# TensorE's instructions pinned to the order of the source in a three-block transformer kernel

## The chip, the cores and the metric

The program runs on one core of one Trainium2 chip. The metric is the device time of one execution in microseconds (us). It is launched once, takes its inputs from HBM and leaves one output of 256 x 1024 fp32 there. The engines are called by the profile's names: PE is TensorE's matmul, PEld its weight loads, DVE VectorE, ACT ScalarE, POOL GpSimd, and SP the queue that issues nearly all loads. "LIN" is used below for the matmuls of lines 217 to 219.

## The reference, cut to what matters

All of it is fp32, batch 1, 256 tokens, model width 1024. A first block takes `x` and a modulation vector:

```python
hn = _rmsnorm(h, norm1_g) * (1.0 + scale1) + shift1
y_ssm = _mamba2_mixer(hn @ w_z, hn @ w_xbc, hn @ w_dt, ...) @ w_ssm_out      # chunked scan, 32 heads
y_nsa = _nsa_mixer(hn @ w_q, hn @ w_kc, ..., hn @ w_gn, ...) @ w_nsa_out     # compressed, selected, window branch
merged = jax.nn.sigmoid(hn @ w_gs) * y_ssm + jax.nn.sigmoid(hn @ w_ga) * y_nsa
h = h + gate1 * (merged @ w_o)
hn2 = _rmsnorm(h, norm2_g) * (1.0 + scale2) + shift2
h = h + gate2 * _hier_moe(hn2, ...)                                          # 32 experts, 2 for each token
```

Two more layers follow on that result. Layer 0 is grouped-query attention with a context stream of 256 tokens of its own and a gated feed-forward part (2816 wide, with a convolution of three taps). Layer 1 is latent attention with a second feed-forward part. A last norm gives the output. The modulation vectors of all layers are products of a silu-ed vector with wide matrices (`w_ada`, `ada_w`).

## The kernel before, in words

**Products.** Weights are fp32 in HBM. `split_weight` (L188) loads 256 KB pieces into the ring `raw` (14 buffers), ACT rounds a piece to `whi` (L198), DVE takes the rest `wlo` (L199), four buffers each. `mm3` (L214) then makes three matmuls for each product: `whi` by hi (L217), `wlo` by hi (L218), `whi` by lo (L219). `lin_fm` (L221) yields after each 24 of these, `lin_tm` (L247) after 12 wider ones or so. Products with the modulation weights (`ada_quad`, L385) go straight from `raw` in fp32: one unit is eight matmul records of L391, in four column tiles.

**How the stages are written.** Each stage is a Python generator that yields the cost of a unit. `weave` (L137) traces units of side chains among the units of a main one, by shares: beside `tanh_gates` (L1012) go the scan `ssd` (share 0.7, then 0.6), the sparse attention `nsa` (0.35) and the modulation (0.3); beside `ssd_gate` the sparse attention (0.55). `drain` traces what is left of a chain with nothing beside it. So the source has an order: the order in which instructions are traced. Between two yields a generator's instructions stand together, with nothing of another chain among them.

**What orders the instructions.** Tile's scheduler takes the traced program, keeps the data dependencies, and gives each engine an order of its own by a model of the times: where the next instruction in the source's order is not ready by that model, a later one goes first. PE's sequence in the profile is thus not the source's. PSUM is cut into rings by `banks` (L122): in the first block `aux` has two banks.

**Places that the prediction speaks of**, in the order of the program:

- `first_block` (L1021): `project_tm` (L581) is the second projection; then `project_xbc` with `nsa_prepare`.
- `ssd` (L654): for each of four groups and two chunks, transposes (L685), two pairs of matmuls (L704, L705), L713 or L722 and L728, and L735. L704 and L705 are followed by an exponential (L707, ACT) and a product (L708, DVE) that L735 reads. The last one and a half of its eight rounds are drained before the z projection.
- `nsa_compress` (L830) ends in one unit with L855, L864, L873, L880, each reading what DVE made of the one before. `nsa_cmp_probs` (L887) is one unit: L894, a copy, transposes L900, a softmax on DVE and ACT (L901 to L917), transposes L921.
- `nsa_attend` (L925): scores L941, transposes L973, products L980 and L986. Its last 15 units are drained after the z projection (L1053), then comes the product with `w_nsa_out` beside `ssd_norm` (L764; L769, a chain on DVE and POOL, L519).
- `layer0_ctx_in` (L1651): `load_fm` loads 1 MB of the context into the buffer that the last `y_lo` leaves, and transposes it (L362). This is traced after the last product with `w_ssm_out` and before the first with `w_o` (L1079 to L1083).
- `square_sums`, `rstd_bcast`, `spread` (L477 to L521): a norm, as L489 (sums of squares), a copy (L492), L494, DVE, POOL (L507), DVE (L516), L519, all in one unit.
- `router`, `experts` (L1093, L1381), beside them the context's attention; `experts_rest` (L1396) is a conditional block.
- `layer0_x_attend` (L1690): `final_norm`, projections, heads (L1571), attention (L1710, L1490, L1498).
- `layer1_x` (L1828): `mla_in`, twice two `mla_norm` (L1738: ACT, DVE, POOL, DVE, then transposes L1751), `mla_kv_heads` (L1794) and `mla_q_heads` (L1812), beside them the attention (L1848).
- The feed-forward parts are plain runs of `lin_fm`; `finish` (L1869) is the last norm.

Of the kernel before, what the change touches and what calls it, by code (L numbers as in the profile page):

```python
# [79 lines left out]
# The quads of ada columns that are made beside the router and beside layer 0's attention.  # L80
Q2, Q3 = (0,), (1, 2)
# The rings that hold weights loaded ahead for the experts, before and after the phase's buffers are free.
ROOM = ("raw", "k4"), ("raw", "k4", "Q", "raw", "k4")
# How much of a side chain goes beside each step of the main one.
# [4 lines left out]
# The experts by their rank in number of tokens: the order of the units (rank of group, half) and their blocks.  # L89
# [3 lines left out]
# The 8 KB buffers: those of the second part lie where what the first part keeps there is done early.  # L93
# [5 lines left out]
class Kernel:  # L99
# [21 lines left out]
    @contextmanager  # L121
    def banks(self, **bufs):  # L122
        """The eight PSUM banks, cut into rings for one part of the program."""
        with self.tc.tile_pool(name="psum", bufs=1, space=bass.MemoryType.PSUM, reuse_waits="tile") as self.psum:
            self.psum_bufs = bufs
            yield

    @contextmanager
    def phase(self, **bufs):
        """Buffers that live for one part of the program."""  # L130
        with self.tc.tile_pool(name="phase", bufs=1, reuse_waits="tile") as p:
            self.phase_pool, self.phase_bufs = p, bufs
            yield
        self.phase_pool, self.phase_bufs = None, {}

    @staticmethod
    def weave(main, *fills):  # L137
        """main with units of each (generator, share) among its own, by their TensorE time. A fill that yields None
        waits for main."""
        done, spent = 0.0, [0.0] * len(fills)  # L140
        for cost in main:
            yield cost
            done += cost
            for i, (g, share) in enumerate(fills):
                while spent[i] < share * done:
                    try:
                        c = next(g)
                    except StopIteration:
                        spent[i] = float("inf")
                        break  # L150
                    if c is None:
                        spent[i] = share * done
                        break
                    spent[i] += c
                    yield c
# [14 lines left out]
    def passing(self, name, tag):  # L170
        """A constant that is needed only once."""
        which, a, n = self.cst_at[name]
        t = self.sb(tag, [P, n], name=name)
# [8 lines left out]
    # ---------------------------------------------------------------- weights  # L182
# [5 lines left out]
    def split_weight(self, view):  # L188
        """(hi, lo) of each block of 128 rows of a view [128, n, cols]."""
# [14 lines left out]
    def flush(self):  # L204
        """Evictions are traced after the next weights' split, which TensorE waits for."""
# [15 lines left out]
    def lin_fm(self, W, c0, ncols, act, evict, k0=0, nk=None, more=False):  # L221
        """out^T: features on partitions. W [K, N] in DRAM; act (hi, lo) [128, nk, 256]."""
# [24 lines left out]
    def lin_tm(self, W, c0, ncols, act, evict, chunk=512):  # L247
        """out: tokens on partitions."""
# [25 lines left out]
    # ---------------------------------------------------------------- set-up  # L274
# [73 lines left out]
    def load_fm(self, src, h, tag, eng):  # L348
        """[256, 1024] rows of DRAM -> feature-major h [128, 8, 256]."""
# [16 lines left out]
    # ---------------------------------------------------------------- adaLN  # L366
# [11 lines left out]
    def take_bias(self, stg, dst):  # L378
        """The bias into dst [128, slots, 48], to which the products are added."""
# [5 lines left out]
    def ada_quad(self, W, q, dst, rsel):  # L385
        """Columns 2048q..2048q+2047 of silu(c) @ W onto dst [128, slots, 48]."""
# [17 lines left out]
    def ada_start(self, p):  # L404
        """Shift and scale of the first norm for half of the features, in the order of ada1."""
# [20 lines left out]
    def first_act(self, rb):  # L426
        """The first norm and the first two chunks of the token-major projection, by halves of the features as the
        modulation comes in."""
# [47 lines left out]
    # ---------------------------------------------------------------- norms  # L476
    def square_sums(self, h, nt, st, gain=None):  # L477
        """Sums of squares over features (32 times them) into the two columns of st: the column tiles of TensorE add up
        a quarter each."""
# [17 lines left out]
    def rms_bcast(self, h, nt, dim):  # L497
        """1/rms over features, one column per token, on all partitions (PSUM [128, 256])."""
# [11 lines left out]
    def spread(self, r, n):  # L510
        """Columns of r, one value per token, along the free dimension of all partitions."""
# [11 lines left out]
    def modulation(self, gain, ada, slot, vs, vsc):  # L523
        """gain * (1 + scale) and shift, [128, 8] each."""
# [15 lines left out]
    # ---------------------------------------------------------------- first block: projections  # L540
# [26 lines left out]
    def rope(self, x, nh, t, outs):  # L567
        """x [128, nh, 64] token-major, half-split rotation; written to each of outs."""
# [12 lines left out]
    def project_tm(self, act, pss):  # L581
        """dt, q, k/v, gates of the first block, tokens on partitions; the first two chunks are in pss."""
# [8 lines left out]
    def conv_silu(self, dst, ps, wname, bname, m, nm, taps):  # L591
        """Causal depthwise convolution over tokens, then silu."""
# [20 lines left out]
    # ---------------------------------------------------------------- SSD  # L613
# [40 lines left out]
    def ssd(self):  # L654
        """The chunked scan; y (with the skip) replaces the x channels. Yields where TensorE would wait."""
# [90 lines left out]
    def ssd_gate(self, act, sums):  # L746
        """y * silu(z), and its squares summed by group into sums [2][128, 2, 256]."""
# [35 lines left out]
    # ---------------------------------------------------------------- NSA  # L783
# [141 lines left out]
    def nsa_attend(self):  # L925
        """Selected and window branches (causal both: every block is chosen and the window spans the sequence)."""
# [79 lines left out]
    # ---------------------------------------------------------------- first block  # L1006
    def sigmoid(self, out, x):
        """By tanh, whose table is the exponential's too."""
# [3 lines left out]
    def tanh_gates(self, act, c0, sg):  # L1012
        """tanh(x / 2): the sigmoid is half of one more."""
        def ev(m, ps):
            self.A.activation(sg[:, m, :], ps, AF.Tanh, scale=0.5)
        yield from self.lin_fm(self.I["w_in"][0], c0, D, act, ev)

# [3 lines left out]
    def first_block(self, rb):  # L1021
        V, A, T, I = self.V, self.A, self.T, self.I
        h = self.h
        act, pss = self.first_act(rb)
        self.mark("tm")
# [66 lines left out]
    # ---------------------------------------------------------------- mixture of experts  # L1092
    def router(self, h):  # L1093
# [35 lines left out]
        def top(x):  # L1129
            """softmax over the 8 columns; its sorted values and their places."""  # L1130
# [55 lines left out]
        # experts by their number of tokens: place of each expert and expert of each place  # L1186
# [67 lines left out]
    def one_hots(self, d, cols):  # L1254
        """For positions 256 d + cols: token x position, by first and second choice, [128, 2, n] per half of tokens."""
# [10 lines left out]
    def expert_gather(self, d, tag, n=256):  # L1266
        """The normalised tokens at positions 256 d.., features on partitions."""
# [15 lines left out]
    def expert_weights(self, part, experts):  # L1283
        """One part of the experts' weights, 256 rows of gate or up or 256 columns of down each."""
# [21 lines left out]
    def expert_block(self, xg, d, q, experts, sizes):  # L1306
        """The 128 positions 256 d + 128 q..: one expert's, or several experts' in the column tiles of TensorE."""
# [42 lines left out]
    def expert_spread(self, d, q):  # L1350
        """What takes the block's rows back to the tokens, position x token, and the rows' weights."""
# [29 lines left out]
    def experts(self):  # L1381
        """The two experts with the most tokens have 128 positions each, the next two 64, the others 32."""
# [13 lines left out]
    def experts_rest(self):  # L1396
        """Tokens beyond those positions: blocks of 32 from position 1536."""
# [8 lines left out]
    def final_norm(self, h, gain, mod, tag):  # L1406
        """The next norm (hi, lo) of h normalised with its gain, and what brings h itself there."""
# [8 lines left out]
        # with m the mean square of h, the mean square s / m of the normalised h, plus eps, times m: both norms at once  # L1416
# [17 lines left out]
    # ---------------------------------------------------------------- second block  # L1434
    def axial(self, x, nh, cos, sin, out):
        """x [128, nh, dim] token-major -> out; cos, sin [128, dim] (signs and gains inside)."""
# [13 lines left out]
    def attend(self, S_fn, V_fn, nkt, scale, hi, lo, s_tag, o_tag, ready=None, room=None):  # L1450
        """Softmax attention of 16 heads in pairs, 256 queries; out^T into (hi, lo). Scores run two steps ahead."""
# [87 lines left out]
    def gqa_heads(self, pr, is_x, c0, nh, t_done):  # L1539
        """Norm and rotation of the heads in columns c0.. of pr, by halves of the tokens; t_done(t, c0) takes them."""  # L1540
# [34 lines left out]
    def gqa_project(self, act, is_x, qT, kT, tags):  # L1575
        """Keys and values first; each piece's heads are finished under the next piece's products."""
# [161 lines left out]
    def mla_norm(self, src, col, n, gain, dst, t0):  # L1738
        """rms-normalised columns, transposed to features on partitions with the gain; dst (hi, lo)."""
# [17 lines left out]
    def mla_in(self, act, col0, n):  # L1757
        """Columns col0.. of the products into latents, by halves of the tokens."""
# [7 lines left out]
    def mla_latent(self, pin, is_x):  # L1766
        """Normed latent (transposed) and shared keys from the 288 columns of keys and values."""
# [13 lines left out]
    def mla_kv_heads(self, ck, kr, c, is_x, vm, kc):  # L1781
        """Keys and values of heads 4c.. into kTm, vm; kc [128, 2, 4, 96] is room for the keys."""
# [86 lines left out]
    def finish(self):  # L1869
        """The last norm, tokens on partitions."""  # L1870
# [22 lines left out]
    def run(self):  # L1893
        with self.tc.tile_pool(name="sb", bufs=1) as self.pool:
# [26 lines left out]
            with self.phase(k4=4, m=3, fg=2, hT=2):  # L1921
                with self.banks(lin=2, S=2, aux=2, acc=2):
# [10 lines left out]
                    self.mark("experts rest")  # L1933
                    self.experts_rest()
                with self.banks(lin=4, fl=1, aux=2, acc=1):
# [9 lines left out]
                    self.drain(self.layer1_x())  # L1945
                    self.finish()
# [31 lines left out]
```

## Time and profile before

| | before |
|---|---|
| times of three runs | 1762.91, 1765.79, 1771.38 us; median 1765.79 |
| span of the profiled execution | 1765.9 us |
| PE busy, share of the span | 1690.6 us, 96% |
| PEld busy | 1379.4 us, 78% |
| DVE busy | 1272.3 us, 72% |
| ACT busy | 917.8 us, 52% |
| HBM read | 378.00 MB, 215 GB/s over the span |
| mean granted TensorE clock | 0.981 |

The page gives no time of the profiled execution beside its span; the span is 0.1 us above the median of the runs. PE counts as busy while any matmul record is open, and the records overlap: a LIN matmul of 256 columns has a record of 0.28 us and the next one starts 0.12 us after it, so a short wait between two matmuls can lie inside a busy stretch. [...]

### The profile page before, as it was taken

The page shows a single profiled execution, that of the slowest core. Times are in us where ns is not written, and L with a number is a line of the kernel's source. Part 1 is how long each engine was busy: PE and PEld are TensorE (multiplying, and loading weights), DVE is VectorE, ACT ScalarE, POOL GpSimd, SP SyncE. Part 2 cuts the span into 40 slices and gives each one's busy share as a digit, 9 for nine tenths or more (in the row PEclk, how much of TensorE's full clock was granted, in tenths as well). Part 3 has the DMA queues.
Part 4 walks back from the last instruction along what each step waited for, and adds up shares of the span by engine and source line. Part 5 has one row for each costly group of instructions (what it writes and reads, how often), then busy time and mean ns, then how long its engine had stood idle before and what let it go on. Part 6 is the DMA issues. An engine that isn't in the chain of part 4 may idle for free. (4 is left out here: it accounts for less than half of the span.)

```text
span 1765.9 us, 36466 instructions
## 1 busy us (share of the span) xinstructions
PE 1690.6 (96%) x12980; PEld 1379.4 (78%) x12980; DVE 1272.3 (72%) x3070; ACT 917.8 (52%) x1901; POOL 42.4 (2%) x48
## 2 busy tenths in 40 slices
PE   7999999999999999999999898999999989999998
PEld 3898777767876578888887554688999866789997
DVE  3997687675667768757756466968777788777876
ACT  2666446863443544534434252656665566556654
POOL 0000000100001000000000001000000000000000
PEclk8999999999999999999999988999999999999999
DMA  9756956849966997998999886234566432246662
GB/s 321 212 150 195 322 175 191 253 133 306 317 201 207 323 318 240 329 328 268 325 347 346 258 299 229 90 122 138 178 183 183 141 120 72 59 141 183 180 186 72
DMA packets 344962, 381.54 MB, mean 216 GB/s; under 512 B 27353, under 2 KB 298454, under 8 KB 344774
## 3 DMA queue, kind: packets, MB, share of 16 engines
q1 hardware_dynamic: 339456, 376.47, 67.2%
q10 hardware_dynamic: 5174, 1.97, 0.4%
q8 instruction: 104, 1.70, 0.4%
q0 software_dynamic: 144, 0.71, 0.1%
q14 instruction: 84, 0.69, 0.1%
HBM read 378.00 MB, written 1.05 MB: 215 GB/s over the span
## 5 line engine op out<-in xcount | busy, mean ns | idle before, releaser
L198 ACT CAST whi<-raw 128x512 fp32r<-128x512 f32 (+2 forms) x752 | 453.9, 610 | 383.9 <-PE lin L219 219.5
L199 DVE TENSOR_TENSOR wlo<-raw,whi 128x512 fp32r<-128x512 f32 (+2 forms) x752 | 502.4, 678 | 161.5 <-ACT whi L198 148.6
L217 PE MATMUL lin<-XA,whi 128*128 128x256 f32 x768 | 220.1, 287 | 1.7 <-ACT XA L465 1.7
L219 PE MATMUL lin<-XA,whi 128*128 128x256 f32 x768 | 219.0, 286 | 0.0
L218 PE MATMUL lin<-XA,wlo 128*128 128x256 f32 x768 | 218.9, 285 | 0.0
L217 PE MATMUL lin<-A,whi 128*128 128x256 f32 x576 | 168.4, 292 | 2.7 <-DVE k L598 1.9
L218 PE MATMUL lin<-A,wlo 128*128 128x256 f32 x576 | 163.5, 284 | 0.0
L217 PEld LDWEIGHTS lin<-XA,whi 128*128 128x128 f32 x768 | 149.3, 194 | 2.6 <-ACT XA L465 2.5
L218 PEld LDWEIGHTS lin<-XA,wlo 128*128 128x128 f32 x768 | 149.2, 194 | 0.7 <-issue 0.4
L219 PEld LDWEIGHTS lin<-XA,whi 128*128 128x128 f32 x768 | 148.9, 194 | 0.3
L217 PEld LDWEIGHTS lin<-A,whi 128*128 128x128 f32 x576 | 109.9, 191 | 33.8 <-issue 14.1
L219 PE MATMUL lin<-A,whi 128*128 128x256 f32 x448 | 127.7, 285 | 0.0
L217 PE MATMUL lin<-CA,whi 128*128 128x256 f32 x416 | 122.0, 293 | 0.3 <-ACT whi L198 0.2
L218 PE MATMUL lin<-CA,wlo 128*128 128x256 f32 x416 | 118.2, 284 | 1.1 <-DVE wlo L199 1.1
L219 PE MATMUL lin<-CA,whi 128*128 128x256 f32 x416 | 117.9, 283 | 0.0
L218 PEld LDWEIGHTS lin<-A,wlo 128*128 128x128 f32 x576 | 110.1, 191 | 0.9 <-issue 0.7
L1621 ACT ACTIVATE cv<-lin,vecs 128x256 f32<-128x256 f32 x132 | 73.9, 560 | 63.0 <-PE lin L219 52.7
L219 PE MATMUL lin<-XB,whi 128*128 128x256 f32 x352 | 99.4, 286 | 0.1
L1622 DVE SCALAR_TENSOR_TENSOR cv<-lin,vecs,cv 128x255 f32<-128x255 f32 x132 | 63.3, 480 | 49.4 <-ACT cv L1621 49.1
L217 PE MATMUL lin<-XB,whi 128*128 128x256 f32 x352 | 98.7, 283 | 0.0
L218 PE MATMUL lin<-XB,wlo 128*128 128x256 f32 x352 | 98.4, 283 | 0.0
L217 PEld LDWEIGHTS lin<-CA,whi 128*128 128x128 f32 x416 | 79.2, 190 | 15.5 <-issue 6.5
(534 smaller groups left out, 3835.0 us busy)
## 6 DMA issues: line engine op xcount, KB each, us to landing
raw<-in_ffn_w_up_dram SPq DMA_DIRECT2D x264, 256.0 KB
raw<-in_ada_w_dram SPq DMA_DIRECT2D x192, 256.0 KB
raw<-in_ffn_w_down_dram SPq DMA_DIRECT2D x132, 256.0 KB
raw<-in_w_in_dram SPq DMA_DIRECT2D x112, 256.0 KB
wx<-in_w_exp_gate_dram SPq DMA_DIRECT2D x112, 256.0 KB
wx<-in_w_exp_up_dram SPq DMA_DIRECT2D x112, 256.0 KB
wx<-in_w_exp_down_dram SPq DMA_DIRECT2D x112, 256.0 KB
raw<-in_w_ada_dram SPq DMA_DIRECT2D x96, 256.0 KB
```

The costliest lines, as they stand in the source:

```text
L198: self.A.copy(hi, raw)
L199: self.V.tensor_tensor(lo, raw, hi.bitcast(F32), OP.subtract)
L217: mm(out, whi, ahi, start=first, stop=False, skip_group_check=True)
L218: mm(out, wlo, ahi, start=False, stop=False, skip_group_check=True)
L219: mm(out, whi, alo, start=False, stop=last, skip_group_check=True)
L1621: A.activation(acc, ps, AF.Identity, bias=self.v(f"fb{i}", m), scale=self.v(f"fw{i}1", m))
L1622: V.scalar_tensor_tensor(acc[:, 1:], ps[:, 0:TOK - 1], self.v(f"fw{i}0", m), acc[:, 1:], OP.mult, OP.add)
```

## The change

A method `pin` opens and closes a region in which the scheduler has to issue PE's instructions in the order in which they were traced. The other engines' orders, and the DMA queues', stay the scheduler's. The region opens after `first_act`, ahead of the second projection, is closed around the conditional block `experts_rest`, and ends ahead of `finish`. No unit, share, buffer or operation differs. The diff takes out the comments and docstrings too; these lines are left out here.

```diff
+    def pin(self, on=True):
+
+        if on:
+            self.pinned = self.tc.manual_schedule(engines={mybir.EngineType.PE})
+            self.pinned.__enter__()
+        else:
+            self.pinned.__exit__(None, None, None)
...
         act, pss = self.first_act(rb)
+        self.pin()
         self.mark("tm")
...
                     self.mark("experts rest")
+                    self.pin(False)
                     self.experts_rest()
+                    self.pin()
...
                     self.mark("L1")
                     self.drain(self.layer1_x())
+                    self.pin(False)
                     self.finish()
```

## Rows read from the trace of the kernel before

**Rows 1.** The page, by engine: busy us, share of the span, instructions.
```profile
PE 1690.6 (96%) x12980; PEld 1379.4 (78%) x12980; DVE 1272.3 (72%) x3070; ACT 917.8 (52%) x1901; POOL 42.4 (2%) x48
```
**Rows 2.** Windows: stretch, length, PE, PEld, DVE, ACT, POOL busy us (count), clock, DMA share, GB/s.
```profile
44.10:1721.80 1677.70, 1622.51 (x12482) 1327.93 (x12481) 1228.32 (x2970) 884.82 (x1838) 40.05 (x41) 0.98 0.69 217
1280.30:1324.40 44.10, 44.10 (x370) 44.10 (x369) 34.48 (x68) 28.03 (x54) 0.00 (x0) 1.00 0.61 183
```
**Rows 3.** Timeline of PE, first block: start, us, line, out<-in, tile shape, form, count.
```profile
187.45 0.64 PE L848 MATMUL acc<-raw,blk 128*32 128x128 f32 x16
187.91 1.02 PE L391 MATMUL fl<-raw,stat 128*32 128x512 f32 x2
188.86 0.50 PE L704 MATMUL aux<-k,tri_r 128*128 128x512 f32 x1
189.29 1.06 PE L391 MATMUL fl<-raw,stat 128*32 128x512 f32 x6
190.28 0.39 PE L217 MATMUL lin<-A,whi 128*128 128x256 f32 x1
...
212.90 1.06 PE L391 MATMUL fl<-raw,stat 128*32 128x512 f32 x8
213.90 0.38 PE L217 MATMUL lin<-A,whi 128*128 128x256 f32 x1
```
**Rows 4.** Timelines of SP and PE, the context's load.
```profile
474.58 0.37 SPq L354 DMA_DIRECT2D x_tm<-in_ctx_dram  x1
...
479.79 0.71 PE L362 MATMUL aux<-ident,x_tm 128*128 128x128 f32 x5
```
**Rows 5.** Timeline of PE, two norms; in brackets the idle time before, and its releaser.
```profile
488.79 0.67 PE L519 MATMUL aux<-k,ones 128*128 128x256 f32 x2 [0.34 <-DVE k L516]
...
1409.71 0.61 PE L494 MATMUL aux<-ones,sqsum 128*128 128x1 f32 x4 [0.53 <-DVE sqsum L492]
1411.96 1.19 PE L519 MATMUL aux<-k,ones 128*128 128x256 f32 x2 [1.65 <-DVE k L516]
```
**Rows 6.** Timeline of PE, the compressed branch's softmax; window of the tile scmp: DVE, ACT busy.
```profile
230.60 0.38 PE L900 MATMUL aux<-ident,scmpT 128*128 128x128 f32 x2
...
238.10 0.44 PE L921 MATMUL aux<-ident,scmp 128*128 128x128 f32 x2
...
231.00:238.10 7.10, 0.00 (x1) 0.01 (x1) 3.93 (x7) 0.63 (x1) 1.00 0.80 256
```
**Rows 7.** Windows of line L217 alone: stretch, length, PE busy (count), PEld busy.
```profile
271.10:285.80 14.70, 3.98 (x13) 2.45 (x13) 1.00 0.65 196
359.00:388.00 29.00, 2.71 (x9) 1.70 (x9) 1.00 0.36 112
```
**Rows 8.** Windows of line L391 alone.
```profile
271.10:285.80 14.70, 3.17 (x16) 0.45 (x16) 1.00 0.65 196
359.00:388.00 29.00, 2.10 (x8) 0.29 (x8) 1.00 0.36 112
```
**Rows 9.** Timelines of ACT and PE, layer 1's latents.
```profile
1423.38 0.40 ACT L1762 COPY pin<-lin 128x288 f32<-128x288 f32 x1
1426.31 0.30 PE L1751 MATMUL aux<-ident,junk 128*128 128x128 f32 x1 [0.66 <-DVE junk L1747]
...
1433.55 0.48 ACT L1762 COPY pin<-lin 128x384 f32<-128x384 f32 x1
1436.73 0.33 PE L1751 MATMUL aux<-ident,junk 128*128 128x128 f32 x1 [0.38 <-DVE junk L1747]
```
**Rows 10.** Waits of PE: who for whom, us in total, times, longest.
```profile
PE acc L1339 <- DVE hT L1328: 2.9, 4, 1.8
```
**Rows 11.** Windows, as in Rows 2, around falls of the granted clock.
```profile
1005.00:1011.16 6.16, 4.57 (x38) 2.12 (x36) 3.04 (x8) 0.69 (x1) 0.00 (x0) 1.00 0.03 9
1011.16:1028.23 17.07, 12.69 (x52) 4.56 (x54) 5.10 (x15) 8.67 (x19) 1.66 (x2) 0.50 0.70 237
1410.52:1417.35 6.83, 4.27 (x14) 3.44 (x15) 4.45 (x11) 2.15 (x5) 0.70 (x1) 0.50 0.02 6
```

## The prediction

> **What bounds the kernel now.** I read the page's busy times first, then the windows, then the waits and timelines. PE is busy for 1690.6 of 1765.9 us, the next engine, DVE, for 72% [rows 1]. From the second projection's stretch to the last slice it is busy for 1622.5 of 1677.7 us [rows 2]: the sum of all its visible waits there is 55.2 us. Removing every wait could not win more than that, while added ones have no such end. The feed-forward parts show what a stretch without waits looks like: busy for 44.1 of 44.1 us [rows 2]. They are plain runs of one generator with nothing beside it, so their order is the source's already; those 380 us or so neither win nor lose.
>
> Three things in the rows show that PE's order is not the source's. L391's unit of eight is cut in 2 and 6 with L704 between [rows 3]. LIN of the z projection and L391, 3 x 13 matmuls and 16 records, run inside the last rounds of the scan, which the source drains with nothing beside them [rows 7, 8]. LIN of the next product fill the time until the context has landed, which the source puts behind it [rows 4]. The amount of PE's work stays; what the change alters is how much of it lies under other engines' chains. PE waits at the first instruction in the source's order that isn't ready, and all behind it wait too. So I go through the places where the source has a chain with no other PE work between its links and the trace has some.
>
> **The change part by part.** The sum is against the profiled execution, 1765.9 us, which is the median of the runs within 0.1 us.
>
> *Context load.* The DMA goes out at 474.58, when the last product that reads its buffer's old content is through, and L362 starts at 479.79 [rows 4]: 5.2 us, filled with LIN of `w_o`. In the source L362 stands ahead of those. PE stands for the whole latency: **+5.2**. [...]
>
> *Norms.* Without cover L494 waits 0.53 and L519 1.65 us [rows 5]: 2.2 us that the source has in every norm, for a norm is one unit. With the cover that the scheduler found, L519 waits 0.34 [rows 5]. There are six covered places: the context's first norm, the router's, the scan's, the context's in its feed-forward part, the final norm and the context's in layer 1, 1.6 to 1.9 us each: **+10** (5 to 13).
>
> *Compressed branch.* L900 ends at about 231.0, L921 starts at 238.1 [rows 6]. In these 7.1 us PE had LIN, L391 and scores to do. The chain's own work on that tile is 3.93 us of DVE and 0.63 of ACT [rows 6], 4.6; with three small operations on its sums and the passages between engines, which the rows of the norm show to add a few tenths each, I take 5.5. L855 to L880 and the two L894-to-L900 passages before it are four more round trips of 0.5 to 0.7 (the 0.53 of [rows 5] is one). Together **+8** (5 to 10).
>
> *Scan.* In the last rounds, 14.7 us long, 39 LIN at 0.12 (4.7) and 16 L391 (3.2) lie between the links [rows 7, 8]; 7.9 us of later work, which the source has behind them. The chains (exponential, product, the two banks of `aux`) need part of it: I take 4. Six rounds woven into the gate projections have two or three of the scan's units in a row; half to one us each for the bank to come free, 4 in all. **+8** (0 to 15).
>
> *Sparse attention's drain.* Between 359 and 388, 27 LIN (3.2) and 8 L391 (2.1) are pulled ahead [rows 7, 8]. The last 15 units follow each other in the source: **+5** (0 to 6).
>
> *Latents of layer 1.* From the eviction's start to the first transposes are 2.9 us (1423.38 to 1426.31) and 3.2 us (1433.55 to 1436.73), of which 0.66 and 0.38 show as waits, the rest is LIN of the next products [rows 9]. In the source nothing stands there, so +2.3 and +2.8; the second halves of the tokens and the transposes of the first heads, with the same kind of chain, I put at 4 more, the three further rounds of heads at 1 each: **+12** (6 to 18).
>
> *Router, experts, grouped-query heads.* L1339 waits 2.9 us in four of its ten blocks [rows 10]; a few LIN after L1357 hide it in the others. 0.5 us each there, 3 for the heads' chain ahead of L1571. The experts' weights come at full DMA load, so part may cost nothing: **+6** (0 to 15).
>
> *What goes.* A run of two L391 takes 0.95 us (187.91 to 188.86) and the other six 0.99, an undivided unit of eight 1.00 [rows 3]. A cut costs 0.94 us. Counted along PE's timeline there are some 85 runs for 64 units ([rows 3] shows one cut); 12 of the cuts lie where PE was not waiting anyway: −11 (0 to −20). Waits that the scheduler's order itself made: −3. **−14**.
>
> *Clock.* After the stretch in which PE was busy for 4.57 of 6.16 us the granted clock fell to 0.50 for 17.1 us; inside the norm of [rows 5], after PE had stood twice, for 6.8 us [rows 11]. These are two of seven such stretches between 1000 and 1570. Five of the new waits are of that size (context load, softmax, the two latents, one drain). A stretch of 6.8 us at half the clock costs at most 3.4 if PE works all through; in this one it was busy for 4.27 of 6.83. I take 2 each: **+10** (0 to 25).
>
> Sum: 5.2 + 10 + 8 + 8 + 5 + 12 + 6 = 54.2; less 14, plus 10: **+50**, 1816 us. No DMA is issued by PE, SP's order stays, and `raw` runs up to 14 pieces ahead; loads are late only where PE frees buffers late. While PE stands, ACT and DVE can round at most two units of weights ahead (four buffers of `whi`), and where PE is the bound that gives nothing back. Around the norms DVE is what is late next.
>
> [...] The rows give 0.94 us for a cut of L391, and L848's 16 records, in column tiles too, take 0.46 (187.45 to 187.91) in front of L391 [rows 3]. [...]
>
> **The rivals.**
>
> *Whole units win* (faster). All 20 cuts join (−19), the source's LIN units of 24 (2.9 us) cover most chains, and of the waits only the context load and the softmax stay (+11); with −10 of the scheduler's own misplaced waits out of the 55.2: about −18, 1748 us. For it: the source does put a LIN unit between most links. Against it: the places above have none. It decides from the point where the added waits are under 25 us.
>
> *Nothing to measure* (flat). The scheduler takes the source's order where it can, so the orders are close; added 25, saved 20: 1770. For it: most LIN groups stand whole in the timeline. Against: the 39 LIN and 16 L391 in the scan's end.
>
> *The clock tips more often* (slower still). If the waits bring a dozen further stretches at 0.50, at 3.4 us each instead of five at 2, and the bounds of scan and latents are reached: 54 + 13 − 5 + 41, about +100, 1868 us or more.
>
> That PE's order stays what it is cannot be: the drained rounds have an order of their own in the source.
>
> **How the numbers follow.** Forecast 0.67, whole units 0.12, flat 0.11, clock 0.10. Ends of the forecast from the terms' bounds: all the low ones with the full 20 saved come to about −5, which asks for all at once; I take 1775 to 1870. About 0.5% (9 us) is what a measurement can tell from no change. The range for 8 in 10 is 1762 to 1868, which takes in the flat case and half of the last. Faster 0.12, within 0.5% 0.11, slower 0.77.
>
> **What would show it.** PE's waits between 44 and the last slice grow from 55 to some 100 us. L362 waits about 5 us for the context's DMA in one piece, with no LIN of `w_o` before it. L921 waits 4.6 to 6 us. L391 stands in runs of eight. L1751 waits 2 to 3 us twice. New stretches of granted clock 0.50 between 240 and 500. The feed-forward parts keep their lengths. The prediction is wrong if these waits are there and the span is not longer (then PE was not the bound where I put them), or if they aren't there since other work of the source's order lies between.

## The result, and the profile after

The changed kernel takes 1953.94 us (median of 4 runs, 1951.5 to 1957.23) against 1765.94 before (4 runs): ratio 1.106, 95% interval 1.1035 to 1.1081. That is 188 us slower. The forecast had the sign right and the size wrong: +50, with a range that ended at 1868.

The page of the kernel after, with the row that answers to [rows 1] and the granted clock in 40 slices:

```profile
span 1953.2 us, 36450 instructions
PE 1726.0 (88%) x12980; PEld 1415.1 (72%) x12980; DVE 1290.2 (66%) x3070; ACT 919.5 (47%) x1897; POOL 43.5 (2%) x48
PEclk9999889999989898999999977988999988999999
```

The same 12980 records of PE. PE stood for 75.3 us before (1765.9 − 1690.6) and stands for 227.2 after: +152. Its busy time grew by 35.4. Together that is the span's growth, 187.3.

The windows of the kernel after, stage by stage, columns as in [rows 2]: first block; context load, `w_o` and router; experts; final norm and layer 0's attention; the start of layer 0's remainder; its feed-forward part with layer 1's context; layer 1's attention; layer 1's feed-forward part; and, last, a piece from inside a feed-forward part, which answers to the second of [rows 2].

```profile
87.70:531.10 443.40, 395.81 (x3047) 315.52 (x3047) 292.98 (x741) 218.75 (x479) 13.76 (x14) 0.94 0.63 196
531.10:622.80 91.70, 75.89 (x478) 58.45 (x477) 54.03 (x147) 35.79 (x69) 3.38 (x4) 0.93 0.59 189
622.80:1120.50 497.70, 454.38 (x3955) 361.26 (x3956) 312.70 (x732) 189.92 (x388) 7.24 (x5) 0.96 0.89 282
1120.50:1277.20 156.70, 117.37 (x652) 69.27 (x652) 102.07 (x250) 68.19 (x149) 10.38 (x8) 0.83 0.53 175
1277.20:1402.40 125.20, 111.82 (x812) 103.11 (x809) 89.36 (x200) 72.42 (x150) 2.87 (x4) 0.92 0.42 127
1402.40:1601.60 199.20, 179.45 (x1349) 172.38 (x1348) 138.70 (x293) 106.53 (x209) 2.86 (x5) 0.94 0.50 147
1601.60:1702.00 100.40, 87.05 (x431) 58.48 (x430) 68.62 (x190) 52.02 (x123) 0.00 (x0) 0.95 0.18 57
1702.00:1944.40 242.40, 232.38 (x1872) 226.60 (x1870) 174.45 (x342) 137.27 (x261) 0.70 (x1) 0.98 0.48 142
...
1421.30:1465.40 44.10, 44.10 (x369) 44.10 (x369) 34.45 (x67) 27.75 (x53) 0.00 (x0) 1.00 0.63 181
```

Against the same stages of before, of which three in the same columns (first block, experts, layer 0's attention):

```profile
83.00:474.30 391.30, 385.56 (x3044) 306.69 (x3043) 290.93 (x752) 221.67 (x482) 12.11 (x14) 1.00 0.70 223
...
551.70:1007.70 456.00, 443.62 (x3945) 353.62 (x3946) 308.90 (x732) 187.63 (x387) 7.56 (x5) 1.00 0.97 308
1007.70:1146.30 138.60, 126.39 (x654) 69.68 (x652) 99.23 (x251) 67.18 (x149) 10.55 (x8) 0.89 0.59 198
```

| stage | before, us (idle) | after, us (idle) | longer by |
|---|---|---|---|
| first block | 391.3 (5.7) | 443.4 (47.6) | 52.1 |
| context, router | 77.4 (3.4) | 91.7 (15.8) | 14.3 |
| experts | 456.0 (12.4) | 497.7 (43.3) | 41.7 |
| layer 0's attention | 138.6 (12.2) | 156.7 (39.3) | 18.1 |
| layer 0, start of the rest | 115.4 (7.0) | 125.2 (13.4) | 9.8 |
| layer 0's feed-forward part | 177.2 (7.7) | 199.2 (19.8) | 22.0 |
| layer 1's attention | 84.9 (2.8) | 100.4 (13.4) | 15.5 |
| layer 1's feed-forward part | 233.3 (4.0) | 242.4 (10.0) | 9.1 |

No stage is the culprit; all of them lose, and mostly by idle time. The stages add up to 182.6 us; the other 4.7 lie ahead of the first window. Only the inside of a feed-forward part is as dense as before (44.10 of 44.10 us). Who PE waits for, in the kernel after (a selection, in the order of the list; us in total, times, longest):

```profile
PE aux L1580 <- DVE pr L1457: 16.8, 2, 10.8
PE aux L704 <- DVE k L698: 15.9, 11, 2.7
PE aux L519 <- DVE k L516: 15.4, 9, 3.2
PE aux L1760 <- DVE junk L1756: 13.2, 5, 2.9
PE acc L1507 <- DVE pT L1501: 10.0, 12, 2.0
PE aux L1335 <- DVE k L1332: 9.2, 7, 2.8
PE lin L217 <- ACT XB L211: 7.8, 8, 1.1
PE aux L921 <- DVE scmp L917: 5.8, 1, 5.8
PE acc L1348 <- DVE hT L1337: 4.6, 8, 2.5
PE aux L1821 <- DVE room L1457: 3.7, 4, 1.5
```

All are links of a chain through DVE and ACT: turning of the heads (L1580), the scan's cumulative sum (L704), the broadcast of a norm (L519), latents (L1760), attention's product with V (L1507), the experts' hidden rows (L1335, L1348; the latter was [rows 10]), the first down product of a feed-forward part (L217), the softmax (L921), and layer 1's heads (L1821). Put down to what ended it, PE's idle time up to the last product grew by 116.5 us at DVE (35.8 to 152.3), 25.6 at ACT (20.6 to 46.2) and 9.8 at DMA (10.1 to 19.9, of which 5.1 is L362's wait for the context). Lines behind L1018 are 9 higher than before.

The rows that answer to [rows 3, 4, 6, 9] in the timelines of PE and SP of the kernel after:

```profile
189.30 1.04 PE L391 MATMUL fl<-raw,stat 128*32 128x512 f32 x8
...
256.19 1.09 PE L921 MATMUL aux<-ident,scmp 128*128 128x128 f32 x4 [5.80 <-DVE scmp L917]
...
531.43 0.37 SPq L354 DMA_DIRECT2D x_tm<-in_ctx_dram  x1
...
536.48 3.84 PE L362 MATMUL aux<-ident,x_tm 128*128 128x128 f32 x16 [5.08 <-DMA x_tm<-in_ctx_dram]
...
1574.84 0.41 PE L1760 MATMUL aux<-ident,junk 128*128 128x128 f32 x2 [2.57 <-DVE junk L1756]
```

L391 stands in whole units, L362 waits out the context's latency in one piece.

The clock: windows ahead of two falls of the granted clock and after them, which answer to [rows 11]:

```profile
173.70:180.55 6.85, 4.88 (x52) 3.80 (x49) 2.90 (x5) 2.54 (x5) 0.00 (x0) 1.00 0.74 217
180.55:183.96 3.41, 3.11 (x26) 1.57 (x26) 1.89 (x4) 1.66 (x3) 0.00 (x0) 0.51 0.32 109
...
1194.37:1201.19 6.82, 4.55 (x26) 3.16 (x26) 2.05 (x4) 2.79 (x4) 0.00 (x0) 1.00 0.56 193
1201.19:1218.26 17.07, 5.59 (x24) 2.29 (x20) 11.89 (x32) 4.77 (x12) 3.41 (x2) 0.50 0.00 1
```

After a stretch in which PE was busy for 4.88 of 6.85 us (a wait of 2.27 us ahead of L704 begins in it) the granted clock is at the lower of the two levels that both traces show, 0.50, for 3.4 us (0.51 over the window); around the longest wait, 10.82 us, for 17.07. There are 40 stretches at this level after (235 us) against 9 before (71 us). PE was busy inside them for 184.2 and 54.3 us. If all of that work takes twice as long, 92 and 27 us of it are excess: +65. In the trace after, LIN of 256 columns follow each other every 0.120 us at a granted clock of 1.00 and every 0.213 in these stretches (medians); by that pace 80 and 24 us are excess: +57. Without the excess the busy time fell by 22 to 30, of which L391 is 20 (its groups were busy for 95.0 us, now 74.7); the rest was not followed. So **+152 idle, +57 to +65 clock, −22 to −30 work = +187**. The clock's term is an estimate from these figures, not measured by itself; the run with filled waits below shows that such a part is there.

### The profile page after: what moved, and what is told of

Read it like the earlier page. It is cut to its first block, busy times and chain, and to the rows that moved or that the text cites. A ratio compares the mean times of both kernels' runs of the same rounds, so it can differ in the third digit from the quotient of the medians.

```text
span 1953.2 us, 36450 instructions
## 1 busy us (share of the span) xinstructions
PE 1726.0 (88%) x12980; PEld 1415.1 (72%) x12980; DVE 1290.2 (66%) x3070; ACT 919.5 (47%) x1897; POOL 43.5 (2%) x48
## 5 line engine op out<-in xcount | busy, mean ns | idle before, releaser
L217 PE MATMUL lin<-XA,whi 128*128 128x256 f32 x768 | 221.4, 288 | 2.2 <-ACT XA L465 2.2
L217 PE MATMUL lin<-A,whi 128*128 128x256 f32 x576 | 171.4, 298 | 5.2 <-DVE k L598 5.2
L217 PEld LDWEIGHTS lin<-XA,whi 128*128 128x128 f32 x768 | 150.7, 196 | 3.9 <-ACT XA L465 3.4
L217 PEld LDWEIGHTS lin<-A,whi 128*128 128x128 f32 x576 | 113.7, 197 | 38.1 <-issue 23.7
L219 PE MATMUL lin<-A,whi 128*128 128x256 f32 x448 | 129.7, 290 | 0.0
L217 PE MATMUL lin<-CA,whi 128*128 128x256 f32 x416 | 123.5, 297 | 1.1 <-ACT CA L465 1.1
L217 PE MATMUL lin<-XB,whi 128*128 128x256 f32 x352 | 101.8, 289 | 7.8 <-ACT XB L211 7.8
L219 PE MATMUL lin<-XB,whi 128*128 128x256 f32 x352 | 102.2, 290 | 1.1 <-DVE XB L212 0.5
L1631 DVE SCALAR_TENSOR_TENSOR cv<-lin,vecs,cv 128x255 f32<-128x255 f32 x132 | 63.4, 480 | 49.9 <-ACT cv L1630 49.7
L217 PEld LDWEIGHTS lin<-CA,whi 128*128 128x128 f32 x416 | 81.3, 195 | 17.4 <-issue 6.8
```

The costliest lines, as they stand in the source:

```text
L217: mm(out, whi, ahi, start=first, stop=False, skip_group_check=True)
L219: mm(out, whi, alo, start=False, stop=last, skip_group_check=True)
L1631: V.scalar_tensor_tensor(acc[:, 1:], ps[:, 0:TOK - 1], self.v(f"fw{i}0", m), acc[:, 1:], OP.mult, OP.add)
```

## Experiments

**Parts of the change alone.** Theory A says that each place loses by itself; B, that the order upsets queues and rings of the whole program; C, that the clock is most of it.

```
p_first:    first_block(rb); + self.pin(False)          # no pin() later
p_experts:  + self.pin() ahead of the router; self.pin(False) ahead of experts_rest; no other
p_layers:   self.pin() behind experts_rest only
```

> TensorE keeps the source's order in the first block alone (second projection to the end of layer 1's mixer); from the context load on it is free again, as before. Theory A (each place loses by itself: its source has a chain of evictions with nothing else for TensorE between the links): the loss is what the stretch showed under the full change, 443.4 us against 391.3, so +52 to +57 and 1818 to 1823 us, nothing lost later. Theory B (the order upsets the other queues and the weights' ring of the whole program): parts that are not pinned lose too, so over +65. Theory C (mostly the clock, which tips once waits of many stages add up): clearly less than +50.

> TensorE keeps the source's order from the context load and router to the last expert that is woven, and nowhere else. Theory A: the two stretches showed 91.7 against 77.4 us and 497.7 against 456.0 us under the full change, so +54 to +58 and 1820 to 1824 us. Theory B: over +65. Theory C: clearly less than +50. My forecast had priced router, experts and grouped-query heads together at +6 and the context load at +5, which would be 1777.

> TensorE keeps the source's order from layer 0's attention to layer 1's end alone. Theory A: the stretches under the full change add up to +76 (20.0 + 3.6 + 6.2 + 22.0 + 15.5 + 9.1), so 1838 to 1846 us, and the three partial kernels together lose the 188 us of the full change within 10 us. Theory B: the three together lose more than 200. Theory C: they lose less than 150. My forecast had the latents (12) and a share of the heads here, some +20, so 1786.

Measured: 1840.55 us (ratio 1.0395, 1.0367 to 1.0424), 1813.63 (1.0252, 1.0224 to 1.0279) and 1838.23 (1.0395, 1.0375 to 1.0416), beside 1767.13. That is +73.4, +46.5 and +71.1, 191 together against 188. Only the third is what theory A said. The first lies over the 65 that was set for theory B, the second under the 54 of theory A. The windows show why: `first_block` ends behind the context's load and `w_o`, not ahead of them as the expectation had it. In the first kernel 5.2 us are lost ahead of the first window, 57.4 in the first block and 10.9 at the context and router, 73.5 of the 74.4 that its trace is longer; in the second kernel the context and router are +5.3 in place of +14.3. Windows of p_first (first block; context and router; experts, no longer pinned), then of p_layers (layer 1's attention and feed-forward part):

```profile
88.20:536.90 448.70, 399.46 (x3048) 318.36 (x3047) 293.04 (x741) 218.30 (x479) 13.75 (x14) 0.94 0.62 194
536.90:625.20 88.30, 77.01 (x488) 58.74 (x487) 54.18 (x148) 36.25 (x71) 3.38 (x4) 0.94 0.61 196
625.20:1081.00 455.80, 442.99 (x3946) 353.65 (x3946) 309.19 (x732) 187.64 (x387) 7.52 (x5) 1.00 0.97 308
```

```profile
1481.60:1582.00 100.40, 87.06 (x431) 58.49 (x430) 68.54 (x190) 52.04 (x122) 0.00 (x0) 0.95 0.18 57
1582.00:1824.40 242.40, 232.38 (x1872) 226.60 (x1870) 174.47 (x342) 137.35 (x261) 0.70 (x1) 0.98 0.48 142
```

Where the pin ends the loss ends (455.8 us for the experts, 456.0 before), and layer 1 costs the same to a tenth whether the rest is pinned or not (100.40 and 242.40 in the windows after). With that, and with 9.8 us of added waits for DMA in the whole kernel, B is out. C, as a cause that needs many stages, is out too; the clock's part falls inside each stage.

**Cover put into the source, under the pin.** Three edits that place other work of the same program between two links:

```
c_combine:  attention: combine(i) one step later, behind the next scores
c_scan:     xdt, xw built behind the decay segments, not ahead of them
c_expert:   yield COST * {(0,"g"): 0, (0,"u"): 0, (3,"u"): 3}.get((i, n), 1)
c_all:      the three together
```

> The changed kernel (pinned throughout), and in every attention but the sparse one the product with V moved behind the next step's scores, in the source. Theory A (waits come from what stands next in the source): the waits at that product, 16.9 us under the change (6.2 beside the experts, 4.9 and 1.6 in layer 0, 3.3 and 0.9 in layer 1), mostly go, 12 to 17 us less than the changed kernel's 1954: 1937 to 1942. Rival (the chain's length sets the time, whatever stands between): another link waits instead, 1950 to 1958.

> The changed kernel, and in the scan the decay segments are made ahead of the scaled input, in the source. Theory A: VectorE no longer makes the scaled input while TensorE stands at the cumulative sum, whose waits under the change are 18.9 us in 20 places: 10 to 18 us less, 1936 to 1944. Rival (VectorE's work per round sets the pace, whatever the order): the wait moves to the products with the scaled input, 1950 to 1958.

> The changed kernel, and the fill that an expert's block of gate and up products calls for is called for after its last product (3 units of cost there, none after the first two), the block's total being the same. Theory A: a unit of fill of some 7 us stands ahead of the turning of the hidden rows in most blocks, whose waits under the change are 9.2 us in 7 places: 6 to 10 us less, 1944 to 1948. Rival (the fill then lacks somewhere else, or the down products' waits of 5.6 and 5.9 us grow): 1952 to 1960.

> The changed kernel with the three edits together. Theory A: the gains add up, 28 to 45 us, and some half-clock time goes with the waits (the change added 35 us of TensorE's busy time beside 152 of idle time): 1905 to 1926 us. Rival (chain lengths set the time): 1948 to 1960.

Measured, beside 1767.96: 1936.43, 1947.04, 1945.13 and 1944.69. By the medians c_combine and c_expert do about what theory A asked for, c_scan falls between the two ranges, and c_all, 9.3 us under the change, is far from theory A's 28 to 45. The traces say less. Waits of PE in c_combine, then c_scan:

```profile
PE aux L1820 <- DVE room L1457: 11.0, 8, 2.0
...
PE acc L1507 <- DVE pT L1501: 4.0, 6, 1.8
```

```profile
PE aux L713 <- DVE k L709: 7.5, 3, 2.9
PE aux L695 <- DVE k L689: 7.0, 4, 3.0
```

The wait at the edited link shrank in each: L1507's from 10.0 to 4.0, the cumulative sum's (now L695) from 15.9 to 7.0, L1335's beside the experts from 9.2 to 1.9. But other links took over part of it or all: in c_combine layer 1's heads went from 3.7 to 11.0 (now L1820); in c_scan the state product (L713) waits 7.5 that it had not, and the scan's waits together went from 19.3 to 24.9; in c_expert the fill's weight splits wait 5.3. PE's idle time, 218.6 us up to the last product, became 213.4, 222.9, 216.1 and 216.3. The rival was right on the waits of c_scan and c_expert. In c_combine a part stayed won: idle time in layer 0's attention, taken from the first projection behind the norm (1139.7 to 1277.2 us after), went from 29.7 to 24.7. A stage that no edit touches differs by about 2 us (the first block's idle time is 47.6 us after, 49.2 in c_combine, 49.0 in c_expert).

The larger part of what the medians gained is clock: half-clock time is 205, 228, 211 and 225 us against 235, and in c_combine's trace idle time fell by 5.2 us, busy time by 15.2. (c_scan's trace is of its slowest execution, 1953.91, so it does not hold the median's gain.) Some of that isn't the edits' own: in layer 0's attention, which c_expert does not touch, idle time is 29.7 us after and 30.1 there, half-clock time 41.0 and 28.4, and the stretch 137.5 and 132.0. So 5 us of one stretch come and go with the same waits, and the three gains (17.5, 6.9, 8.8) did not add up in c_all (9.3). The changed kernel itself was not run again beside these.

**Cover by work that hangs on nothing.** In the kernel before, the heads' chain of layer 0 had L391 beside it: 24 records in one piece at 1089.1. Put back:

```
gqa_heads, x only, ahead of the transposes of t = 0:
+   for _, _ in zip(range(4), self.x_fill): pass        # four whole ada units
run:  self.mix(self.layer0_x_attend(), (ada, 0.2 -> 0.1))
```

> The changed kernel, and in layer 0's attention four whole units of the modulation's columns (4 us of TensorE's work that depends on nothing here) are put in the source right ahead of the turning of each half of the heads, where TensorE waited 10.8 and 6.0 us; the rest of these units is spread at half the share. The amount of work is the same. Theory A (what stands between the links in the source sets the wait): the two waits fall by about 4 each, 6 to 12 us less than 1954, with some half-clock time. Rival (the wait moves to another link of the same chain, or the units wait for their weights, 16 loads of 256 KB): within 4 us of 1954.

Measured: 1941.34 (beside 1769.22; after was 1953.94). The timeline of PE:

```profile
1201.33 3.97 PE L391 MATMUL fl<-raw,stat 128*32 128x512 f32 x28
1206.00 1.70 PE L391 MATMUL fl<-raw,stat 128*32 128x512 f32 x4 [0.69 <-DMA raw<-in_ada_w_dram]
1211.42 0.63 PE L1583 MATMUL aux<-ident,pr 128*128 128x128 f32 x4 [3.71 <-DVE pr L1457]
```

The wait of 10.8 us is 3.7, with 0.7 more for a weight load inside the cover; L1580's two waits (16.8) are 4.8 at what is now L1583, idle time of the stretch 29.7 → 21.1, its length 137.5 → 129.2 (132.0 to 134.6 in the pinned kernels c_expert, c_scan and p_layers, which leave it alone). Inside its stretch this cover didn't move the wait; theory A held there. The median's 12.6 us, a little over its 6 to 12, are not all the edit's: over the whole kernel idle time fell by 5.1 us only, as the start and the first block, which the edit leaves alone, had 5 more, and half-clock time fell from 235 to 199.

**The clock.** Thrown-away products of the identity ahead of the long waits, under the pin:

```
hold(ps, n): n x matmul(ps, ident, ident)   # ps is overwritten by the real product
ahead of L704, L921, L1580, L1507, L1335, L1348, L1760, L519
```

> The changed kernel, and some 500 products of the identity with itself (128x128, thrown away) stand right ahead of the instructions that wait longest under the pin: the scan's cumulative sum, the compressed branch's probabilities, the heads' turning, the products with V, the experts' hidden rows, the latents' norms and the broadcast of every norm. They only fill waits; nothing of the dependency chains changes. Theory C (part of the loss is the clock that falls in waits: half-clock time grew by about 146 us and TensorE's busy time by 35): half-clock time falls by 60 us or more and the kernel is 10 to 35 us faster than 1954. Theory A alone (only the waits count): 0 to 40 us slower, by the dummies that don't fit into a wait.

Measured: 1938.47 (ratio to before 1.0963, 1.0947 to 1.0979), 15.5 us faster than the change, doing more. Its page:

```profile
span 1943.2 us, 38365 instructions
PE 1788.9 (92%) x13948; PEld 1498.2 (77%) x13948; DVE 1290.8 (66%) x3070; ACT 920.0 (47%) x1897; POOL 45.3 (2%) x48
PEclk9999999999998899999999979999999999999999
```

Idle time fell by 73 us (227.2 to 154.3) and half-clock time from 235 to 113. The products' three groups were busy for 99.6, 21.9 and 6.9 us, 128 at most, so up to 55 of them lay outside waits, and yet the kernel gained: what the fill won back of the clock is at least 15 us and, with those 55, at most some 70. The 113 us at half clock that are left, against 71 before, are not in that number. C is a part, not the whole.

The same idea on the kernel before, unpinned, six products ahead of the broadcast of each norm and 20 behind the experts, then from layer 0 on alone:

> The kernel before, without a pin, and thrown-away products that depend on what the norms have just made, six ahead of the broadcast of each norm and 20 ahead of the first sums after the experts, where half-clock stretches of 6.8, 6.8, 6.8 and 17.1 us stand in the trace before. Theory C: most of these stretches stay at full clock, 5 to 15 us faster than 1766. Theory A alone: 0 to 6 us slower, by the dummies' time where no wait covers them.

> The kernel before, without a pin, with six thrown-away products ahead of the broadcast of each norm from the second layers' start on, and nowhere else. In the last run these same products kept layer 0's and layer 1's norms at full clock (the stretches from layer 0's attention on came out 3.8, 1.1, 1.6 and 2.2 us shorter, one 0.9 longer), while the stretches up to the experts' end lost 10 and the 40 products after the experts 5. Theory C: 4 to 9 us faster than the kernel before, 1757 to 1762. Theory A alone: within 3 us of it.

Measured: 1775.69 (1.0042, 1.0027 to 1.0057) and 1765.05 beside 1768.65 (0.9982, 0.9969 to 0.9994). The first, 7.4 us slower, missed both ranges: the 20 products started 3.55 us into the wait and then held PE for over 11. The second is the only kernel here ahead of the one before, by 3.6 us. That lies between theory A's 3 and theory C's 4 to 9, decides little between them, and is under the 0.5% named in the prediction. Half-clock time fell from 71 to 30 us.

**Finer steps, and the edits without a pin.**

```
g_fine:  projections: yield 0.66 after each 128 rows, not n * 0.66 after four
u_all:   the edits of c_all on the kernel before, no pin
```

> The changed kernel, and the projections give way after each block of 128 rows (6 products) rather than after four (24), at a quarter of the cost each, so the other chains' steps stand more evenly among them in the source. Theory A, in the form that bursts are the trouble (two links of a chain one behind the other after a long unit, then a long unit again): the waits of the scan, the sparse attention, the experts and the latents shrink, 20 to 60 us less than 1954. Rival (each link's chain is longer than any unit and waits at the same places): within 10 us of 1954.

> No pin at all, but three edits of the source's order that are meant to give chains cover under the pin: in attention the product with V comes one step after the turned probabilities; in the scan the decay segments are made before the scaled input; the experts' share of fill work is gathered behind the last gate and up product. Theory A: the scheduler finds that cover by itself, so the edits are worth nothing here: 1766 within 6 us. Rival: the order of the source steers the scheduler as well, and these edits gain 10 us or more without any pin.

Measured: 1936.19 (1.0955, 1.0936 to 1.0974) and 1784.99 (1.0083, 1.006 to 1.0107). With finer steps the experts' stretch lost 8.5 us (idle 43.3 to 33.0), and the first block ended 6.1 us earlier (its idle time 47.6 to 41.0). With 17.8 us in all it lies between the two expectations, just under theory A's 20. u_all missed on both sides: the free scheduler's order depends on the source's too, and here the edits cost 18: 13.4 in the experts' stretch, 4.9 in layer 1's attention. Why the first is so large was not followed further.

## Why the prediction was wrong

The mechanism was right: PE stands at the first instruction in source order whose operand isn't there, and all behind it stand too (L362 5.08 us for the context's load, L921 5.80 for the softmax). Two terms were far too small, the dense attentions had no term, and one claim of zero was wrong. Idle time of PE ahead of each place, added up from its timelines:

| term | forecast (bounds) | before → after, us | change |
|---|---|---|---|
| context load | 5.2 | 1.9 → 6.9 | 5.0 |
| norms | 10 (5 to 13) | 17.1 → 30.0 | 12.9 |
| compressed branch | 8 (5 to 10) | 0 → 9.0 | 9.0 |
| scan | 8 (0 to 15) | 0.5 → 19.3 | 18.9 |
| sparse attention | 5 (0 to 6) | 1.5 → 9.1 | 7.6 |
| latents and heads of layer 1 | 12 (6 to 18) | 1.8 → 18.2 | 16.4 |
| router, experts, grouped-query heads | 6 (0 to 15) | 12.9 → 49.7 | 36.9 |
| dense attentions | no term | 7.7 → 32.3 | 24.6 |
| projections (LIN) | 0 | 12.9 → 24.6 | 11.7 |
| the rest | 0 | 4.1 → 10.9 | 6.7 |
| what goes | −14 (0 to −20, and waits −3) | work | −22 to −30 |
| clock | 10 (0 to 25) | 24 to 27 → 80 to 92 | 57 to 65 |

The ten rows of waits sum to 150; the other 2 us of idle time lie ahead of the first products (L340), before the pin.

*The step that failed* is "router, experts, grouped-query heads: +6". It measured 36.9: 17.4 at router and experts (most at L1335, L1348, L1381) and 19.5 at the heads (L1580). With it goes a term that is missing: 24.6 at the scores, turned probabilities and products with V of the dense attentions, which the prediction did not price at all. I had read "a few LIN after L1357 hide it" as if the source put them there. In the source an expert's last gate and up product is often followed at once by the transposes of its result. And the four waits of [rows 10], 2.9 us in all, were taken as the size of the chain, when they were what was left of it after the scheduler had filled it. In a trace from a scheduler a wait shows what could not be hidden, not how long the chain is. The chain must be read from its own instructions. For the heads they stand in the trace before, from the squares on ACT to the first turned half on DVE:

```profile
1083.56 1.14 ACT L1548 ACTIVATE sq<-pr 128x512 f32<-128x512 f32 x2
...
1092.55 0.68 DVE L1448 TENSOR_TENSOR pr<-ta,tb 128x512 f32<-128x512 f32 x1
```

That is 9.7 us, with L391 beside it on PE; under the change the same links take 10.5 (1202.20 to 1212.73), so the chain itself hardly changed, and PE waits 10.8 at its end. The prediction had 3 for it.

*Clock*: forecast as five stretches at 2 us, measured 31 more stretches. In [rows 11] the clock had already fallen around two waits of 0.53 and 1.65 us, to 0.50 for 6.83 us. The rival "the clock tips more often" asked for a dozen stretches and set its time at 1868 or more; it came nearest and got 0.10, and its own price for the waits (67, less 5 for the work that goes, a number that the prediction works out nowhere) was as much too small.

*Scan*: above its upper bound. Most of the wait is at L704, for DVE's segments (L698), in 11 places; the prediction priced `aux`'s banks. That the source has VectorE make the scaled input first is not the whole cause: with that order turned (c_scan) the waits stood at other links of the round and were no smaller. *Sparse attention*, 7.6, is over its upper bound of 6 as well, most of it at L986.

*Projections*: "neither win nor lose" holds inside (44.10 of 44.10 again), not at their ends: the first product of each down projection waits for the eviction of the last column, 8 waits of about 1. The feed-forward parts did not keep their lengths: +22.0 in layer 0, beside layer 1's context, and +9.1 in layer 1.

*Right*: the context load, the compressed branch, the latents (within their bounds), the norms (at the upper bound), and the signs of all terms. The low end of the forecast's terms (about −5) has the context load some 2 us below 5.2. No run shows that: from its issue to L362 it was 5.21 us before (at 266 GB/s) and 5.05 after (at 256). *What goes* was too small: with 58 runs of L391 instead of 81 (the prediction counted some 85), its busy time fell by 20.3 us, 0.88 per run on average. The prediction had put 12 cuts on the path; the busy time fell as if all 23 were. The 20.3 us are about a tenth of what the lost cover cost (152 us of idle time and the clock's 57 to 65).

Of the signs named ahead: L362, L921, L391 and L1760 came out as said, half-clock stretches between 240 and 500 are there (six); PE's waits grew by 152 us rather than by 45, and the feed-forward parts got longer.

## What to carry to other kernels

Ahead of fixing one engine's order, list every chain that leaves that engine and comes back, with the length of the chain from its own instructions, and look at what the source puts behind the leaving instruction; the waits of a scheduled trace are only the remainder. Cover that depends on nothing (the ada units) took 12 of the 16.8 us of two waits away here; moving another link of the same dependent work moved the wait in two of three trials and kept a part of the gain in one. And the added waits were paid for twice here: 152 us as idle time and, by the estimate above, 57 to 65 in the granted clock.

## What was not expected of the hardware

The same pinned stretch, with the same idle time to within half a microsecond (29.7 and 30.1 us), took 137.5 us in the changed kernel and 132.0 in c_expert, by how much of it ran at the lower clock (41.0 and 28.4 us). A change of that size, 5.5 us, can't be read from the median alone in this kernel. Thrown-away products made the pinned kernel 15 us faster, and six ahead of each later norm made the kernel before 0.2% faster (0.9969 to 0.9994).
